# Filter spectra finished inside the convolution, and the gate work moved beside it, in a hybrid encoder layer

## The chip, the core and the metric

The kernel runs on one core of a Trainium2 chip. The metric is device microseconds of that core for one execution; of several executions the median is given. A profile is one further execution, recorded by the hardware profiler; its span runs from the first to the last instruction.

## The reference, cut to what matters

```python
u = rms_norm(h); P = u @ W_in                     # 2048 x 1024 rows; 10 blocks of 512 columns
# Hyena group, 512 channels: v, x1, x2 = conv3(P[:, :1536])
filt = sin_ffn(positions) @ w3 * exp(-t*|deltas|)  # order 2, two directions, length L = 2048
spec = rfft(concat(fwd, 0, flipped bwd))           # length 2L
for o, gate in enumerate((x1, x2)):
    z = gate * (irfft(rfft(z, 2L) * spec[:, o])[:L] + z * skip[o])
# mLSTM group, 4 heads x 128, both directions, from q, k, v, o and gates:
F = cumsum(log_f); m_t = running max; w = exp(...)   # the gates' scans
C = carry_decay * C + we * k v^T                     # states, chunk by chunk
h = (s @ v + inter * q @ C) / max(|den|, exp(-m_t))
# then group norms, output projection, cross-attention (256 memory rows), squared-ReLU MLP
```

## The kernel before, in words

**Numbers.** Most matrix products are done in three passes on split operands (a high and a low part, `wh`/`wl` and `xh`/`xl`, split at L366; the matmuls are L361 to L363, written mm<-xh,wh and so on in the profile). Products of the convolution and of the mLSTM are plain fp32 products, which the profile shows as two matmul records each.

**The convolution** runs as a two-stage transform of 4096 points: a product over 32 or 64 rows of time (`f1`), a store to DRAM that regroups the rows, and a product with one 128 x 128 matrix per pair of frequencies (`dm`). The way back is one product per frequency block (`em`), a store and load through DRAM, and a product with `e2`. Rows go through DRAM in `fs` (filters), `zs` (signal), `zg` (back) and `hd` (finished filter spectra).

**The stages**, in the order of the program (L1845):

1. `filters` (L231), woven with the sweeps over the first columns of W_in: per position pair and order, two products w3 (L177/L185), windows (DVE, POOL), the front (L294: two full 128 x 128 products, L297) and a store to `fs`; then 32 blocks (L323 to L346), each with two `dm` products (L344), copies and a store to `hd`.
2. `hyena` (L812), woven with the remaining sweeps and the `natural` projections: `load1` and `spectrum` (L896) of the signal; then per order 16 frequency steps, each with loads of signal rows and finished spectra (`load2`), copies that double the spectrum over both halves of the partitions (`double`, L862), two `dm` products (L926), the complex product (L928 and L929 on ACT, L930 and L932 on DVE, L931 on POOL) and, one product late, the way back (L892). Then the inverse in eight steps (`load3`, `e2`): for the first order in two column tiles beside each other (L177/L185), for the second as two full products (L949).
3. `mlstm` (L967) begins with the gates: one load of the gate columns (L991), transposes (L998), scans of seven doubling steps each (L1019/L1020), a loop of 62 dependent steps on single values (L1046/L1048), exponentials, and transposes back (L1038, L1052, L1073, L1074). It goes on with 15 backward states (`update`, L1093). Both are woven with `memproj`, the projections of the memory, which holds three of the `natural` blocks.
4. Sixteen chunks (L1162) woven with `memproj`'s end and with the attention; then the MLP.

**What sets the order.** A generator yields after each piece of work; `weave` (L1827) draws from two generators in turn by their yields and the two totals given to it. On top of that a scheduler places each instruction in the queue of its engine, so that the order on an engine differs from the order of the code. Each engine works through its queue in order. `beside` (L173) issues two products that use different parts of the array.

Of the kernel before, what the change touches and what calls it, by code (L numbers as in the profile page):

```python
# [18 lines left out]
L = 2048  # L19
# [8 lines left out]
def shape_constants():  # L28
# [15 lines left out]
    c_win = np.stack([win, winb], 0)  # L44
# [17 lines left out]
    f1h = np.zeros((2, 2, 32, 2, 64))  # L62
    e2h = np.zeros((2, 2, 2, 64, 128))
    for h in range(4):
        f1h[h // 2, h % 2, :, h % 2] = own
        e2h[0, h // 2, h % 2, :, 32 * h:32 * h + 32] = inv
        e2h[1, h // 2, h % 2, :, h::4] = inv
# [9 lines left out]
    for par in range(2):  # L77
# [12 lines left out]
    dm = dm.reshape(32, 128, 128)  # L90
# [7 lines left out]
        "c_f1": f1.transpose(1, 0, 2),  # L98
        "c_f1h": f1h.reshape(128, 128),
        "c_e2h": e2h.reshape(4, 128, 128).transpose(1, 0, 2),  # L100
# [34 lines left out]
class Prog:  # L135
# [37 lines left out]
    def beside(self, first, second):  # L173
        n = self.banks.index(first[0].tensor.name)
        n = self.banks.index(first[0].tensor.name)
        held = self.banks[max(0, n - 4):max(0, n - 2)] if first[0].tensor.name != second[0].tensor.name else []
        b = self.nc.tensor.matmul(*second, start=True, stop=True)  # L177
        for i in reversed(self.nc.cur_bb.bb.instructions[-4000:]):
            own = [x.bass_ap.tensor.name for x in i.ins if getattr(x, "bass_ap", None) is not None]
            for t in [t for t in held if t in own]:  # L180
                held.remove(t)
                self.tc.add_manual_dep(b.ins, i.name, mybir.DependencyInfo(
                    mybir.DependencyClass.Sync, mybir.DependencyReason.DATA), reason="beside")
        with self.tc.high_priority(2000):
            self.tc.keep_in_program_order(self.nc.tensor.matmul(*first, start=True, stop=True))  # L185
# [45 lines left out]
    def filters(self):  # L231
        nc, tc, a = self.nc, self.tc, self.a
        sd = [self.dram(f"fs{o}", (2, 128, 16, CH)) for o in range(2)]
        hd = self.dram("hd", (2, 32, 128, CH))
        sb, ta, tb = self.fsb, self.ta, self.tb
        if True:
# [4 lines left out]
            f1 = sb.tile([128, 2, 128], F32, name="f1")  # L241
            nc.scalar.dma_start(out=f1, in_=a["c_f1"])

            def sine(dst, src, b, fr, first=False):
# [11 lines left out]
                nc.scalar.activation(dst, u if len(dst.shape) == 2 else u.rearrange("p (q j) -> p q j", j=16), AF.Sin)  # L256

            hid = sb.tile([128, 16, 128], F32, name="hid")
            for c in range(4):
# [10 lines left out]
                sine(hid[:, :, 32 * c:32 * c + 32].rearrange("p j q -> p q j"), p2, 2, 3)  # L270
# [23 lines left out]
            def front(e, st, jj, o, js):  # L294
                for p in range(2):
                    pp = self.hy()
                    nc.tensor.matmul(pp, f1[:, p], e[p], start=True, stop=True)  # L297
                    nc.scalar.copy(st[p][:, jj], pp)
                    if jj == 1:
                        nc.sync.dma_start(out=sd[o][p, :, js], in_=st[p])  # L300

            nxt = windows(0)
            for j2 in range(8):
                js = slice(2 * j2, 2 * j2 + 2)
                yield 14
# [17 lines left out]
            def blocks(o, i):  # L323
                p, k = divmod(2 * i, 16)
                dm = sb.tile([128, 2, 128], F32, tag="dm", name="dm", bufs=3)
                d = nc.sync.dma_start(out=dm, in_=a["c_dm"][:, 2 * i:2 * i + 2])
                if o == 0 and i < 3:
                    tc.keep_in_program_order(d)
                t = ta()
                nc.sync.dma_start(out=t, in_=sd[o][p, 8 * k:8 * k + 16].rearrange("(k r) j c -> (r j) k c", k=2))  # L330
                return dm, t

            order = [(o, i) for o in range(2) for i in range(16)]
            q = [blocks(*order[0]), blocks(*order[1])]
            for n, (o, i) in enumerate(order):
                if True:
                    yield 3.4
                    dm, t = q.pop(0)
                    if n + 2 < 32:
                        q.append(blocks(*order[n + 2]))  # L340
                    hs = ta()
                    for m in range(2):
                        pp = self.hy()
                        nc.tensor.matmul(pp, dm[:, m], t[:, m], start=True, stop=True)  # L344
                        nc.scalar.copy(hs[:, m], pp)
                    nc.sync.dma_start(out=hd[o, 2 * i:2 * i + 2].rearrange("k l c -> l k c"), in_=hs)  # L346
# [59 lines left out]
    NAT_AT = (0, 2, 4)  # L406

    def inproj_open(self, es):
# [21 lines left out]
        for i in range(8):  # L430
            mem += ([nat[i // 2]] if i in self.NAT_AT else []) + first[i + 1:i + 2] + second[i:i + 1]
        items = tr[:4] * 2 + tr[4:] + [nat[c] for c in (3, 0, 1, 2)] + tr[4:] + [nat[3]] + mem
# [190 lines left out]
    def memproj(self):  # L623
# [45 lines left out]
        for i in range(8):  # L669
            if i in self.NAT_AT:  # L670
                yield from self.natural(0, (i // 2,))
# [140 lines left out]
    def hyena(self, es):  # L812
        nc, tc, a = self.nc, self.tc, self.a
        hy = self.dram("hy", (3, L, CH)).rearrange("s (n h j) c -> s h n j c", h=4, j=16)
        hq = self.dram("hy", (3, L, CH)).rearrange("s (q j) c -> s q j c", j=16)
        hd = self.dram("hd", (2, 32, 128, CH))
        yh = self.dram("yh", (L, CH)).rearrange("(q j) c -> q j c", j=16)
        sds = [self.dram(f"zs{o}", (32, 2, 4, 16, CH)) for o in range(2)]
        gds = [self.dram(f"zg{o}", (32, 2, 4, 16, CH)) for o in range(2)]

        def by_time(t, s, js):
            for h in range(4):
                nc.sync.dma_start(out=t[32 * h:32 * h + 32], in_=hy[s, h, :, js])

        def by_block(d, i):
            return d[2 * i:2 * i + 2].rearrange("k r h j c -> (r h j) k c")

        def by_pair(d, b, js):
            v = d.rearrange("k r h j c -> h (k r) j c")
            return [(slice(64 * g, 64 * g + 64), v[2 * b + g, :, js]) for g in range(2)]  # L830
# [9 lines left out]
        e2 = sb.tile([128, 4, 128], F32, name="e2")  # L840
        nc.sync.dma_start(out=f1, in_=a["c_f1h"])
        nc.sync.dma_start(out=e2, in_=a["c_e2h"])
        ghy = self.bcast(sb, a["hy_norm_g"], CH, "ghy")
        def load1(j2):
            z = ta()
            js = slice(2 * j2, 2 * j2 + 2)
            by_time(z, 0, js)
            return z

        def load2(o, i):  # L850
            dm = sb.tile([128, 2, 128], F32, tag="dm", name="dm", bufs=2)
            em = sb.tile([128, 2, 128], F32, tag="em", name="em", bufs=2)
            nc.sync.dma_start(out=dm, in_=a["c_dm"][:, 2 * i:2 * i + 2])
            nc.sync.dma_start(out=em, in_=a["c_em"][:, 2 * i:2 * i + 2])
            t, hr, hi = ta(), ta(), ta()
            nc.sync.dma_start(out=t, in_=by_block(sds[o], i))
            src = hd[o, 2 * i:2 * i + 2].rearrange("k (r l) c -> r l k c", r=2)
            nc.sync.dma_start(out=hr[0:64], in_=src[0])
            nc.sync.dma_start(out=hi[64:128], in_=src[1])
            return dm, em, t, hr, hi  # L860

        def double(i, hr, hi):  # L862
            nc.scalar.copy(hr[64:128], hr[0:64])
            if i == 0:
                nc.scalar.copy(hr[64:65, 0], hi[64:65, 0])
                nc.vector.memset(hi[64:65, 0], 0.0)
            nc.vector.tensor_copy(hi[0:64], hi[64:128])

        def load3(o, j2):
            js = slice(2 * j2, 2 * j2 + 2)  # L870
            r = [ta() for p in range(2)]
            for b in range(2):
                for own, d in by_pair(gds[o], b, js):
                    nc.sync.dma_start(out=r[b][own], in_=d)
            gate = ta()
            if o:
                nc.sync.dma_start(out=gate, in_=hq[2, :, js])
            else:
                by_time(gate, 1, js)
# [10 lines left out]
        def back(m, em, y, gs, dst):  # L890
# [3 lines left out]
            if m == 1:  # L894
                nc.scalar.dma_start(out=dst, in_=gs)

        def spectrum(o, j2, z):
            st = [ta() for p in range(2)]
            for jj in range(2):
                pp = [self.hy() for b in range(2)]  # L900
                self.beside(*((pp[b], f1[64 * b:64 * b + 64], z[64 * b:64 * b + 64, jj]) for b in range(2)))
                for b in range(2):
                    (nc.vector.tensor_copy if b else nc.scalar.copy)(st[b][:, jj], pp[b])
            for b in range(2):
                for own, d in by_pair(sds[o], b, slice(2 * j2, 2 * j2 + 2)):
                    (nc.sync if b else nc.scalar).dma_start(out=d, in_=st[b][own])

        q = [load1(0), load1(1)]
        for j2 in range(8):
            yield 3.5  # L910
# [3 lines left out]
        for o in range(2):  # L914
            gd = gds[o]
            nxt = load2(o, 0)
            for i in range(16):
                yield 3.5
                dm, em, t, hr, hi = nxt
                if i < 15:  # L920
                    nxt = load2(o, i + 1)
                gs = ta()
                double(i, hr, hi)
                for m in range(2):
# [8 lines left out]
                    late(lambda m=m, em=em, y=y, gs=gs, dst=by_block(gd, i): back(m, em, y, gs, dst))  # L933
            late(None)
            nxt = load3(o, 0)
            for j2 in range(8):
                yield 3.5 if o else 7.0
# [4 lines left out]
                for jj in range(2):  # L942
                    pp = self.hy()
                    if o == 0:
                        own = [slice(64 * b, 64 * b + 64) for b in range(2)]
                        self.beside(*((pp[own[b]], e2[:, b, own[b]], r[b][:, jj]) for b in range(2)))
                    else:
                        for p in range(2):
                            nc.tensor.matmul(pp, e2[:, 2 + p], r[p][:, jj], start=p == 0, stop=p == 1)  # L949
# [14 lines left out]
                nc.sync.dma_start(out=yh[:, js], in_=sq)  # L964
            late(None)

    def mlstm(self, es):  # L967
        nc, tc, a = self.nc, self.tc, self.a
# [949 lines left out]
```

## Time and profile before

| | |
|---|---|
| median of 3 runs | 3288.78 us (3285.28 to 3291.98) |
| profiled execution | 3292.63 us, span 3290.9 us, mean granted clock 0.975 |
| PE busy | 3097.7 us (94%), 15113 matmul records |
| DVE, ACT, POOL busy | 1971.7 us (60%), 1502.7 us (46%), 1242.2 us (38%) |
| DMA | 655.75 MB, mean 199 GB/s |

Matmuls are pipelined and their ends are modelled, so a busy PE is not PE at its peak. The stages lie in the span as follows: filters to 470 us, signal spectrum to 548, frequency steps and inverses to about 1108, gates, backward states and memory projections to 1346, and the rest (chunks, attention, MLP) to the end.

### The profile page before, as it was taken

The numbers are of one execution on the slowest core, as the hardware profiler recorded it, in microseconds if no ns is written. First come the engines' busy times: TensorE is split into PE (matmuls) and PEld (weight loads), VectorE is DVE, ScalarE is ACT, GpSimd is POOL, SyncE is SP. The second block draws the span as 40 slices with busy tenths as digits, with TensorE's granted clock in tenths as the row PEclk, the third lists the DMA queues.
The fourth block names the chain that finished last, engine by engine and source line by source line (L and its number), as shares of the span: only waits on it lengthen the run. The fifth ranks groups of instructions, "written<-read, shape, count | busy, mean of one in ns | idle before, by whom it ended". The sixth has DMA issues, their size and how long they took to land.

```text
span 3290.9 us, 45063 instructions
## 1 busy us (share of the span) xinstructions
PE 3097.7 (94%) x15113; PEld 2470.2 (75%) x15113; DVE 1971.7 (60%) x3316; ACT 1502.7 (46%) x2842; POOL 1242.2 (38%) x863
## 2 busy tenths in 40 slices
PE   7999999898999996799999998999999999999998
PEld 5656665674667885698988896888788887888876
DVE  7765224535556664676766556665755686565695
ACT  5533445643663343444444435545555543333335
POOL 0122000210222214534433106886756574434483
PEclk9999999999999997899999999999999999999999
DMA  5554998888787679758465526664644475444434
GB/s 188 187 201 148 313 307 257 261 240 249 215 246 231 200 250 309 210 164 262 140 223 196 195 78 225 207 219 160 218 156 157 157 234 166 132 140 140 130 96 163
DMA packets 473903, 655.75 MB, mean 199 GB/s; under 512 B 41278, under 2 KB 253374, under 8 KB 472648
## 3 DMA queue, kind: packets, MB, share of 16 engines
q1 hardware_dynamic: 437796, 594.30, 58.0%
q10 hardware_dynamic: 35876, 58.57, 5.2%
q8 instruction: 120, 1.97, 0.3%
q14 instruction: 111, 0.91, 0.1%
HBM read 437.73 MB, written 214.99 MB: 198 GB/s over the span
## 4 chain that ended last, share of the span: by engine, by line
PE 66%; DMA 14%; DVE 8%; issue 5%; ACT 3%; POOL 2%; SPq 1%; ACTq 0%; DVEq 0%; POOLq 0%
PE mm L361 14%; PE mm L363 13%; PE mm L362 13%; PE hy L363 5%; PE hy L361 5%; PE hy L362 5%; DVE wl L366 2%; PE hy L344 2%; DMA rw<-rows 2%; PE hy L297 2%; DMA wn<-in_w_in_dram 1%; DMA a<-zg 1%; DMA a<-hd 1%; PE hy L177 1%; PE hy L892 1%
## 5 line engine op out<-in xcount | busy, mean ns | idle before, releaser
L366 DVE TENSOR_TENSOR wl<-wn,wh 128x512 fp32r<-128x512 f32 (+1 forms) x364 | 285.9, 820 | 147.8 <-ACT wh L366 144.0
L1499 DVE TENSOR_TENSOR bl<-wr,bh 128x512 fp32r<-128x512 f32 x213 | 239.0, 1129 | 125.2 <-ACT bh L1498 125.1
L1498 ACT CAST ah<-w 128x512 fp32r<-128x512 f32 x284 | 176.5, 623 | 301.2 <-PE hy L362 153.4
L366 ACT CAST wh<-wn 128x512 fp32r<-128x512 f32 (+1 forms) x364 | 209.3, 619 | 211.6 <-DMA wn<-in_w_in_dram 57.9
L931 POOL TENSOR_TENSOR b<-b,a 128x512 f32<-128x512 f32 x64 | 88.6, 1384 | 574.4 <-ACT b L929 406.2
L361 PE MATMUL mm<-xh,wh 128*128 128x512 f32 x640 | 278.0, 436 | 12.3 <-ACT xh L366 5.5
L362 PE MATMUL mm<-xl,wh 128*128 128x512 f32 x640 | 270.2, 423 | 2.2 <-DVE xl L366 1.6
L363 PE MATMUL mm<-xh,wl 128*128 128x512 f32 x640 | 263.2, 411 | 0.0
L1499 DVE TENSOR_TENSOR al<-w,ah 128x512 fp32r<-128x512 f32 x236 | 226.0, 959 | 61.4 <-ACT ah L1498 61.1
L1498 ACT CAST bh<-wr 128x512 fp32r<-128x512 f32 x232 | 143.9, 622 | 231.9 <-PE mm L363 173.9
L363 PE MATMUL mm<-bh,al 128*128 128x512 f32 x576 | 225.4, 394 | 7.6 <-DVE al L1499 4.4
L361 PE MATMUL mm<-bh,ah 128*128 128x512 f32 x576 | 227.0, 394 | 0.9 <-DVE u L1624 0.8
L362 PE MATMUL mm<-bl,ah 128*128 128x512 f32 x576 | 226.1, 393 | 0.0
L361 PE MATMUL mm<-act,wh 128*128 128x512 f32 x512 | 200.4, 395 | 2.9 <-ACT wh L366 2.9
L362 PE MATMUL mm<-act,wh 128*128 128x512 f32 x512 | 200.8, 392 | 0.0
L363 PE MATMUL mm<-act,wl 128*128 128x512 f32 x512 | 199.6, 393 | 0.1
L1355 POOL TENSOR_TENSOR ssum<-ssum,sq 128x512 f32<-128x512 f32 x56 | 80.3, 1433 | 274.5 <-ACT sq L1354 274.5
L361 PEld LDWEIGHTS mm<-xh,wh 128*128 128x128 f32 x640 | 123.0, 192 | 71.8 <-issue 29.9
L361 PE MATMUL hy<-bh,ah 128*128 128x512 f32 x448 | 175.2, 391 | 0.0
L362 PE MATMUL hy<-bl,ah 128*128 128x512 f32 x448 | 174.6, 390 | 0.0
L363 PE MATMUL hy<-bh,al 128*128 128x512 f32 x448 | 174.4, 390 | 0.0
L362 PEld LDWEIGHTS mm<-xl,wh 128*128 128x128 f32 x640 | 122.7, 192 | 53.8 <-issue 26.2
(368 smaller groups left out, 8785.5 us busy)
## 6 DMA issues: line engine op xcount, KB each, us to landing
wr<-hc SPq DMA_DIRECT2D x224, 256.0 KB
w<-in_ff_w_dram SPq DMA_DIRECT2D x176, 256.0 KB
hc<-t SPq DMA_DIRECT2D x128, 256.0 KB
wn<-in_w_in_dram SPq DMA_DIRECT2D x100, 256.0 KB
hc<-q SPq DMA_DIRECT2D x96, 256.0 KB
fs<-a SPq DMA_DIRECT2D x32, 512.0 KB
a<-fs SPq DMA_DIRECT2D x32, 512.0 KB
hd<-a SPq DMA_DIRECT2D x32, 512.0 KB
```

The lines of the kernel that those rows point to most:

```text
L177: b = self.nc.tensor.matmul(*second, start=True, stop=True)
L297: nc.tensor.matmul(pp, f1[:, p], e[p], start=True, stop=True)
L344: nc.tensor.matmul(pp, dm[:, m], t[:, m], start=True, stop=True)
L361: mm(ps, lh, rh, start=start, stop=False)
L362: mm(ps, lh, rl, start=False, stop=False)
L363: mm(ps, ll, rh, start=False, stop=stop)
L366: both = (self.nc.scalar.copy(hi, src), self.nc.vector.tensor_tensor(lo, src, hi.bitcast(F32), ALU.subtract))
L892: nc.tensor.matmul(pg, em[:, m], y, start=True, stop=True)
L931: nc.gpsimd.tensor_tensor(xt, xt, hi[:, m], ALU.mult)
L1355: nc.gpsimd.tensor_tensor(ssum, ssum, sq, ALU.add)
L1498: self.nc.scalar.copy(hi, src)
L1499: eng.tensor_tensor(lo, src, hi.bitcast(F32), ALU.subtract)
```

## The change

1. The front of the filters becomes four 64 x 64 products (two halves of the contraction, two halves of the output, into two banks) instead of two full products; constants and the rows in DRAM are laid out for it. `beside` takes any number of products. Loads and stores by time become two DMAs instead of four, and stores and loads by pair one instead of two or more; the store of the way back becomes two.
2. The 32 blocks at the end of `filters` go, and `hd` and `double` with them. In `hyena`, `load_filter` loads `dm` and the rows of `fs` two steps ahead, and `response` makes the finished spectrum one step ahead, with two copies on ACT and two on DVE per product.
3. The inverse of the second order uses the two column tiles too.
4. The gates become a generator of their own in the weave with the convolution, between `natural(0, (3,))` and `sweep(range(4, 10), 0)`. Two `natural` blocks move from `memproj` into that weave. The totals and some yields of the weaves change.
5. `update`, the sum of the directions and the last scaling of a chunk become fused DVE operations on 128 x 129 or 128 x 128 pieces; the product `ve` of the backward states goes from DVE to POOL.

```diff
 def front(e, st, jj, o, js):
+    pp = [self.hy() for p in range(2)]
+    self.beside(*((pp[p][64 * (p ^ g):64 * (p ^ g) + 64], f1[64 * g:64 * g + 64, 64 * p:64 * p + 64],
+                   e[p][64 * g:64 * g + 64]) for p in range(2) for g in range(2)))
     for p in range(2):
-        nc.tensor.matmul(pp, f1[:, p], e[p], start=True, stop=True)
...
+        def response(i, dm, t):
+            hr, hi = ta(), ta()
+            for m in range(2):
+                pp = self.mm()
+                nc.tensor.matmul(pp, dm[:, m], t[:, m], start=True, stop=True)
+                nc.scalar.copy(hr[0:64, m], pp[0:64])
+                nc.scalar.copy(hr[64:128, m], pp[0:64])
+                nc.vector.tensor_copy(hi[64:128, m], pp[64:128])
+                nc.vector.tensor_copy(hi[0:64, m], pp[64:128])
...
-                            nc.tensor.matmul(pp, e2[:, 2 + p], r[p][:, jj], start=p == 0, stop=p == 1)
+                    self.beside(*((pp[own[g]], e2, r[g][:, jj]) for g in range(2)))
...
-                nc.gpsimd.tensor_tensor(new, old, bc(DC, r), ALU.mult)
-                    nc.vector.tensor_tensor(nv, nv, pc[:, 0:258], ALU.add)
+                    nc.vector.scalar_tensor_tensor(new[:, h], old[:, h], DC[:, r + h:r + h + 1],
+                                                   pc[:, 129 * i:129 * i + 129], ALU.mult, ALU.add)
...
-            weave(p.filters(), s, 230, 200)
+            weave(p.filters(), s, 80, 200)
...
-                            p.sweep(range(4, 10), 0, False), p.natural(0, (3,), p.prep_mem, 2)),
-                      227, 382)
+                            p.natural(0, (3,)), p.gates(), p.sweep(range(4, 10), 0, False),
+                            p.natural(0, (0, 1), p.prep_mem, 2)),
+                      271, 420)
...
-            for _ in take(n, 3):
-                pass
-            weave(n, take(m, 20), 138, 105)
+            weave(n, take(m, 20), 132, 95)
```

In the changed kernel's own lines the transposes of the gates are L965 (columns in), L1005 (ends of the scans), L1019 and L1040/L1041 (back); the three passes are L336 to L338, a pair of `beside` L175/L184, a state's product L1088, a chunk's L1136 to L1176.

On PE, at the gates of the kernel before, this is how the transposes of the loop's result (L1052) and of `G` (L1073) stand:

```order
L362 MATMUL mm_10166<-wl_9794,xh_83 128x256
L363 MATMUL mm_10166<-wh_9793,xl_84 128x256
L361 MATMUL mm_10166<-wh_9793,xh_83 128x256
L1052 MATMUL hy_9016<-ident_60,mm_8951 128x1
L1073 MATMUL hy_9037<-ident_60,G_8924 128x128
L1052 MATMUL hy_9016<-ident_60,mm_8951 128x1
```

On PE, the same place of the changed kernel (`arr` is the gate columns, `ends` the last values of both scans, `mm` the loop's result, `G`, `ed` and `we` what goes back; `e2` marks the first inverse):

```order
L338 MATMUL mm_6154<-wh_5487,xl_84 128x272
L965 MATMUL hy_6195<-ident_60,arr0_6191 128x128
L965 MATMUL hy_6201<-ident_60,arr1_6192 128x128
L1005 MATMUL hy_6257<-ident_60,ends_6251 1x128 x2
L1019 MATMUL hy_6326<-ident_60,mm_6261 128x1
L1040 MATMUL hy_6347<-ident_60,G_6234 128x128
L175 MATMUL hy_6372<-a_6031,e2_2697 64x512
L184 MATMUL hy_6372<-a_6030,e2_2697 64x512
L175 MATMUL hy_6376<-a_6031,e2_2697 64x512
L184 MATMUL hy_6376<-a_6030,e2_2697 64x512
L1019 MATMUL hy_6326<-ident_60,mm_6261 128x1
L1040 MATMUL hy_6347<-ident_60,ed_6342 128x128
```

All of the gates' transposes moved together: before, 345 rows of projections lie between the first and the last of them, now four rows of the inverse.

On DVE, two products of a frequency step of the kernel before:

```order
L930 TENSOR_TENSOR b_3675<-hy_3672,a_3584 128x512
L932 TENSOR_TENSOR b_3675<-b_3675,b_3674 128x512
L930 TENSOR_TENSOR b_3688<-hy_3685,a_3584 128x512
L867 COPY a_3665<-a_3665 64x1024
L932 TENSOR_TENSOR b_3688<-b_3688,b_3687 128x512
```

On DVE, two products of a frequency step of the changed kernel (L914 and L916 are the former L930 and L932):

```order
L914 TENSOR_TENSOR b_3503<-hy_3500,a_3384 128x512
L843 COPY a_3486<-mm_3487 64x512
L844 COPY a_3486<-mm_3487 64x512
L680 MEMSET P_3580 128x1
L916 TENSOR_TENSOR b_3503<-b_3503,b_3502 128x512
L843 COPY a_3486<-mm_3493 64x512
L844 COPY a_3486<-mm_3493 64x512
L914 TENSOR_TENSOR b_3517<-hy_3514,a_3384 128x512
L916 TENSOR_TENSOR b_3517<-b_3517,b_3516 128x512
```

The one copy of 64 x 1024 became four of 64 x 512, which stand between the two operations of the first product and ahead of the second.

On PE, a chunk of the kernel before (L1101 states, L1147 scores, L1185/L1187 the outputs):

```order
L1101 MATMUL hy_10706<-ve_10703,kn_10645 128x129 x2
L1101 MATMUL hy_10710<-ve_10703,kn_10645 128x129 x2
L1147 MATMUL hy_10742<-qn_10721,kk_t_10722 128x128 x4
L1185 MATMUL hy_10762<-va_10502,rw_10505 128x129
L1187 MATMUL hy_10762<-cf_10702,rw_10507 128x129
```

On PE, the same chunk of the changed kernel (`mm<-wl,kt` are passes of `memproj`):

```order
L1088 MATMUL hy_10749<-ve_10742,kn_10683 128x129 x2
L337 MATMUL mm_11117<-wl_11030,kt_10845 128x512
L338 MATMUL mm_11117<-wh_11029,kt_10845 128x512
L1136 MATMUL hy_10910<-qn_10761,kk_t_10762 128x128 x4
L1174 MATMUL hy_10930<-va_10668,rw_10671 128x129
L336 MATMUL mm_11127<-wh_11029,kt_10845 128x512
```

Passes of `memproj` now stand between a chunk's products, up to the fourth chunk.

More of the change, by code (lines that the diff above doesn't have):

```diff
@@ L171, in hy, with beside @@
         return t
[L173 to L177, printed above, removed]
+    def beside(self, *products):
+        names = [p[0].tensor.name for p in products]
+        n = min(self.banks.index(t) for t in names)
+        held = self.banks[max(0, n - 4):max(0, n - 2)] if len(set(names)) > 1 else []
+        b = self.nc.tensor.matmul(*products[-1], start=True, stop=True)
         for i in reversed(self.nc.cur_bb.bb.instructions[-4000:]):
@@ L184, in beside @@
         with self.tc.high_priority(2000):
-            self.tc.keep_in_program_order(self.nc.tensor.matmul(*first, start=True, stop=True))
+            for p in reversed(products[:-1]):
+                self.tc.keep_in_program_order(self.nc.tensor.matmul(*p, start=True, stop=True))
     def dram(self, name, shape):
@@ L322, in filters @@
             late(None)
[L323 to L346, printed above, removed]
         self.fes.close()
@@ L670, in memproj @@
             if i in self.NAT_AT:
[L671 removed]
+                yield from self.natural(0, (self.NAT_AT[i],))
             yield 11
@@ L846, in load1, with load_filter @@
             js = slice(2 * j2, 2 * j2 + 2)
-            by_time(z, 0, js)
-            return z
+            for g in range(2):
+                nc.sync.dma_start(out=z[own[g]], in_=hy[0, g, :, js])
+            return z
+        def load_filter(o, i):
+            dm = sb.tile([128, 2, 128], F32, tag="dm", name="dm", bufs=3)
+            nc.sync.dma_start(out=dm, in_=a["c_dm"][:, 2 * i:2 * i + 2])
+            p, k = divmod(2 * i, 16)
+            t = ta()
+            for g in range(2):
+                nc.sync.dma_start(out=t[own[g]], in_=of_block(fs[o][p, 64 * (p ^ g):64 * (p ^ g) + 64], k))
+            return dm, t
@@ L858, in load2 @@
[L858 to L867, printed above, removed]
+            t = ta()
+            for g in range(2):
+                nc.sync.dma_start(out=t[own[g]], in_=of_block(sds[o][g], 2 * i))
@@ new lines, in load2 @@
+            return em, t
+        def response(i, dm, t):
[7 more added lines that the diff above has]
+                nc.vector.tensor_copy(hi[0:64, m], pp[64:128])
+                if i == 0 and m == 0:
+                    nc.scalar.copy(hr[64:65, 0], pp[64:65])
+                    for r in range(2):
+                        nc.vector.memset(hi[64 * r:64 * r + 1, 0], 0.0)
+            return dm, hr, hi
@@ L894, in back @@
             if m == 1:
-                nc.scalar.dma_start(out=dst, in_=gs)
+                for g in range(2):
+                    nc.scalar.dma_start(out=of_block(dst[g], 2 * i), in_=gs[own[g]])
         def spectrum(o, j2, z):
```

201 lines of the change are left out of this document (97 added, 104 removed).

## The prediction

> **What bounds the kernel now.** I read the windows of the stages first (window, us, then busy time and count of PE, its weight loads, DVE, ACT and POOL, the granted clock, the DMA share and GB/s):
>
> ```profile
> 0.00:470.00 470.00, 435.54 (x1632) 283.70 (x1633) 256.21 (x454) 212.79 (x367) 56.94 (x38) 0.97 0.66 223
> 470.00:548.00 78.00, 72.96 (x298) 47.64 (x297) 31.27 (x46) 31.41 (x47) 0.00 (x0) 1.00 0.88 247
> 548.00:1108.00 560.00, 517.78 (x2533) 372.59 (x2532) 303.15 (x501) 278.44 (x454) 118.69 (x83) 0.97 0.83 243
> 1108.00:1346.00 238.00, 183.61 (x1262) 169.00 (x1260) 130.78 (x377) 93.98 (x230) 80.38 (x66) 0.89 0.79 246
> 1346.00:3291.00 1945.00, 1887.79 (x9392) 1597.23 (x9392) 1250.28 (x1940) 886.07 (x1747) 986.23 (x677) 0.99 0.55 173
> ```
>
> PE is busy for 92 to 97% of four windows; no other engine reaches two thirds, and DMA is short of full. So in these the work on PE sets the time, and a stage is forecast by adding up what PE issues. The fourth is different: 54 us without PE, a clock of 0.89, and DMA at 0.79. Two pieces of it, with the DMA of the whole stage:
>
> ```profile
> 1191.00:1283.00 92.00, 74.14 (x475) 66.52 (x474) 48.13 (x101) 30.90 (x65) 27.73 (x22) 0.87 0.98 304
> 1283.00:1346.00 63.00, 36.73 (x219) 33.25 (x217) 30.39 (x95) 22.90 (x94) 43.99 (x35) 0.78 0.82 259
> DMA packets 55264, 58.64 MB, mean 246 GB/s; under 512 B 5640, under 2 KB 38664, under 8 KB 55244
> ```
>
> At 304 GB/s DMA is full (0.98). In the second piece PE is idle for 26 of 63 us: the first chunks stand alone there.
>
> The prices on PE are distances between starts, not durations, as matmuls overlap. A split pass of 512 columns, one of 256 columns, and a pair of column tiles:
>
> ```profile
> 198.61 0.39 PE L363 MATMUL mm<-xh,wl 128*128 128x512 f32 x1
> 198.84 0.39 PE L361 MATMUL mm<-xh,wh 128*128 128x512 f32 x1
> ...
> 711.01 0.28 PE L362 MATMUL mm<-wl,xh 128*128 128x256 f32 x1
> 711.13 0.28 PE L363 MATMUL mm<-wh,xl 128*128 128x256 f32 x1
> 711.34 0.64 PE L177 MATMUL hy<-a,e 128*64 128x512 f32 x1
> 711.34 0.64 PE L185 MATMUL hy<-a,e 128*64 128x512 f32 x1
> 711.82 0.59 PE L177 MATMUL hy<-a,e 128*64 128x512 f32 x1
> ```
>
> That is 0.23, 0.12, and 0.43 to 0.48 for two records that start together. A full fp32 product, from the chain that ended last (start, us) and the groups of the first window:
>
> ```profile
> 358.26 1.72 PE hy L344 x4
> ...
> L297 PE MATMUL hy<-b,f 128*128 128x512 f32 x128 | 65.5, 624 | 0.0
> L344 PE MATMUL hy<-a,dm 128*128 128x512 f32 x128 | 62.2, 592 | 0.0
> ```
>
> 1.72 us for four records is 0.43 each, 0.86 a product; fronts and blocks have 128 records each.
>
> **The change part by part.** I counted the rows of PE in the order of both programs between the same marks (last filter, last signal product, last inverse, first free chunk) and priced them so.
>
> *Filters, 470 us.* The blocks go from here: 128 x 0.43 = -55. They are not saved: the same 64 products come back as `response`, +55 in the frequency steps. The fronts: 64 products become 64 x 2 quadrant products in groups of four. Two quadrants of one row tile each are the row tiles that already run at once:
>
> ```profile
> 200.75 0.69 PE L177 MATMUL hy<-fw,hid 64*128 64x512 f32 x1
> 200.75 0.69 PE L185 MATMUL hy<-fw,hid 64*128 64x512 f32 x1
> ```
>
> Row tiles start together here into two banks, and column tiles above into one. If four quadrants start together, two full products (1.72) become 0.86: 32 x -0.86 = -27.5; if only two do, 0. I take -27.5, as both halves of the condition show in rows. [...] Sweep passes move on to later stages (141 of them, six steps, at 0.23: -32.3), with 3.4 of transposes. 470 - 55 - 27.5 - 32.3 - 3.4 = 352.
>
> *Signal spectrum, 78 us.* Another 146 sweep passes leave (-33.3). By PE alone 46 would be left; but 12 of the pairs now stand in one run with little beside them, and this stage moves 19 MB at 247 GB/s before, some 16 after, which is 55 us at the rates of 247 to 304 above. I take 55 (48 to 66).
>
> *Frequency steps and inverses, 560 us.* Sweeps and projections moved in, +82.3 (32.3 + 33.3 from above, the rest two `natural` blocks); responses +55; the second inverse in column tiles, 32 x 0.86 to 16 x 0.86, -13.8; transposes +3.4. Sum 687. DMA, at 0.83 here, brings about the same rows (`fs` in place of `hd`) over a longer time, so that waits for it should not grow.
>
> To this comes what the order shows at the gates. They are now all but in one piece on PE, and their DVE rows stand in one piece too. PE works in order, so it waits through the chain from the load to the last transpose, with two inverse pairs (1.7 us) as its only work. The rows, first the load, the scans (L1019/L1020), the loop (L1046/L1048) and the last copy:
>
> ```profile
> 1136.12 0.38 SPq L991 DMA_DIRECT2D gts<-gt  x1
> ...
> 1140.54 0.50 DVE L996 COPY arr<-gts 128x64 f32<-128x64 f32 x4 [3.09 <-DMA gts<-gt]
> ...
> 1145.77 0.29 DVE L1026 TENSOR_TENSOR rw<-rw,ab 128x128 f32<-128x128 f32 x1 [3.18 <-ACT ab L1006]
> ...
> 1146.36 0.28 DVE L1019 TENSOR_TENSOR pad<-pad 64x128 f32<-64x128 f32 x1
> 1146.67 0.29 DVE L1020 TENSOR_TENSOR pad<-pad 64x128 f32<-64x128 f32 x1
> ...
> 1184.28 0.22 DVE L1048 TENSOR_TENSOR mm<-mm,er 1x4 f32<-1x4 f32 x2
> 1184.46 0.23 DVE L1046 TENSOR_TENSOR mm<-mm,er 1x4 f32<-1x4 f32 x2
> ...
> 1190.56 0.69 DVE L1075 COPY cols<-hy 128x512 f32<-128x512 f32 x1 [4.53 <-PE hy L1074]
> ```
>
> Load to data 4.4, and the store that it waits for up to as much again; data to the logarithm's end 5.5 (1140.5 to 1146.0); two scans of 14 steps at 0.31 with their copies, 10.2; the loop, 62 steps at 0.09 (two in 0.18), 5.6; the tail at most 6.5 (1184.7, where the loop ends, to 1191.2, with other work in it), taken at half, 3.3. With 1 for small copies that is 30 to 34, less 1.7, plus 2 for the clock: after a wait matmuls come at half speed, as at the load of `zg`:
>
> ```profile
> 1014.64 3.78 PE L949 MATMUL hy<-a,e 128*128 128x512 f32 x4 [2.76 <-DMA a<-zg]
> ...
> 1018.67 0.43 PE L363 MATMUL mm<-wh,xl 128*128 128x272 f32 x1
> 1018.89 0.43 PE L361 MATMUL mm<-wh,xh 128*128 128x272 f32 x1
> ...
> 1020.73 0.29 PE L362 MATMUL mm<-wl,xh 128*128 128x272 f32 x1
> 1020.86 0.29 PE L363 MATMUL mm<-wh,xl 128*128 128x272 f32 x1
> ```
>
> (0.22 between starts, then 0.13.) [...] I take +34. Before, the same chain stood among projections and cost PE little.
>
> The frequency step on the other engines (busy, mean ns of one):
>
> ```profile
> L903 DVE COPY a<-hy 128x512 f32<-128x512 f32 x16 | 11.0, 687 | 5.2 <-PE hy L185 5.2
> L867 DVE COPY a<-a 64x1024 f32<-64x1024 f32 x32 | 22.1, 690 | 58.0 <-DMA a<-hd 50.0 <-DMA em<-in_c_em_dram 3.6 <-DMA kn<-st 2.8
> ...
> L928 ACT ACTIVATE b<-hy 64x512 f32<-64x512 f32 x64 | 38.2, 596 | 8.2 <-PE hy L926 3.6 <-ACT a L893 1.9 <-DVE b L930 0.6
> L929 ACT COPY b<-hy 64x512 f32<-64x512 f32 x64 | 37.1, 579 | 0.7
> L931 POOL TENSOR_TENSOR b<-b,a 128x512 f32<-128x512 f32 x64 | 88.6, 1384 | 574.4 <-ACT b L929 406.2 <-DVE a L867 135.3 <-DVE wl L366 11.1
> L932 DVE TENSOR_TENSOR b<-b 128x512 f32<-128x512 f32 x64 | 45.2, 707 | 25.5 <-POOL b L931 25.3
> ...
> L892 PE MATMUL hy<-b,em 128*128 128x512 f32 x128 | 67.5, 609 | 12.3 <-DVE b L932 9.5 <-issue 1.7 <-ACT st L802 1.0
> ```
>
> A step gains four copies of 512 columns on DVE (4 x 0.69) and loses one (0.69), +2.1 x 32 = 66 on DVE; ACT gains four at 0.58 and loses one of 64 x 1024. DVE has 257 us free in this window, so this costs nothing as long as the way back (L892) finds its `y`. The chain behind a frequency product is 0.60 + 0.58 + 1.38 + 0.71 = 3.3, with four copies in front of it 6.1; the passes that cover it, some 24 x 0.23 and two products of 0.86, last 7.2. It holds on the mean, and I take +4 for places where it does not. 687 + 34 + 4 = 725.
>
> *Gates, backward states and memory, 238 us.* Its PE work goes from 169.5 by my count to 152, as two projections leave. Its gates are gone from it, chunks 0 to 3 have passes between them, and and a state's work on DVE and POOL is fused. What binds then is the loads: 58.6 MB less the two projections' share, about 53 MB, at 304 GB/s 174 us, and 11 for a start without full queues: 185 (170 by no lean start; 205 if a third of the old idle time stays).
>
> *The rest, 1945 us.* PE fills 97%; a chunk's DVE work is fused, POOL's falls, and neither is waited for by much: -2.
>
> **Sum.** 352 + 55 + 725 + 185 + 1943 = 3260, against 3290.9: -31. The profiled execution took 1.7 more than its span, and the median was 3.9 below that execution: 3260 + 1.7 - 3.9 = 3258. A measurement of this kernel can tell about 0.2% (6.6 us) from no change.
>
> **The rivals.**
>
> *Row tiles take turns at a bank.* Then the fronts cost what they did: +27.5, 3286, no change. [...] 0.15.
>
> *Slower: the frequency step's chain is longer than its cover.* The place is L892's successor and the two DVE operations with copies in between. At 6.1 against 7.2 there is 1.1 us to spare; if ACT's four copies and two evacuations stand ahead of the two operations too (2 x 0.58 more), the chain passes its cover, and 64 products waiting 1.2 each cost 77: 3335. It decides from a chain of 7.2 us on. For it: L892 waited 9.5 us for L932 already, with fewer copies. Against: responses are a step ahead. 0.14.
>
> *The gates' wait is not lost.* While PE waits, DMA brings the weights and rows that the next steps would wait for, and the sweeps that follow have no waits of their own (before, PE was without work for 42 us of that window): -25, 3233. Against it, prefetching is limited by buffers. 0.13.
>
> *The convolution's waits halve.* With more sweep work beside the steps and four loads made into two, half of these 42 us goes, and the fourth stage comes to 170: -40 with some of the spectrum's, 3218. 0.15.
>
> That leaves 0.43 for the forecast. That the change does not do what it says is part of the forecast already: the gates are in the same weave as the convolution, but not beside it on PE.
>
> **How the numbers follow.** The forecast's own bounds are -7 and +11 (spectrum), -15 and +20 (fourth stage), -8 and +4 (gates), together about 3235 to 3283. Reaching to the third and fourth rival and above the first gives 3205 to 3305; the slower rival is left out. Faster by over 0.2%: all but the top of the forecast, both faster rivals and a third of the first, 0.40 + 0.28 + 0.05 = 0.73. Slower: its rival and bits of the first and the forecast, 0.16. No change, 0.11.
>
> **What would show it.** Four records of the front that start together (two by two: first rival). PE idle for 30 to 36 us between the last `natural(0, (3,))` pass and the first inverse, with L1005 waiting for DVE. Waits of L871 (the former L892) for L916 below 15 us in all; above 60, the slower rival. The stage from the last inverse to chunk 5 at 170 to 205 us with a clock above 0.93. PE-bound filters of 352 us. The forecast is wrong if PE keeps full through the gates, or if the spectrum's run of pairs waits longer than 15 us.

## The result and the profile after

The changed kernel takes 3261.32 us (median of 4, 3256.08 to 3272.3) against 3288.79; the ratio is 0.9919, 95% interval 0.9900 to 0.9939. The forecast was 3258. The profiled execution took 3256.08 us, span 3254.4, with a clock of 0.975 as before.

The windows of the same five stages in the changed kernel (columns as before), and the piece of the third that holds the gates:

```profile
0.00:355.00 355.00, 325.37 (x1460) 207.61 (x1460) 241.63 (x441) 161.48 (x284) 58.08 (x38) 0.99 0.55 180
355.00:418.40 63.40, 52.04 (x207) 31.38 (x204) 24.40 (x38) 22.06 (x37) 0.00 (x0) 0.92 0.94 305
418.40:1105.00 686.60, 630.83 (x3079) 454.63 (x3078) 404.55 (x750) 347.44 (x591) 118.69 (x83) 0.96 0.70 202
1105.00:1313.00 208.00, 164.34 (x1106) 152.13 (x1105) 112.12 (x292) 83.53 (x222) 67.33 (x56) 0.87 0.90 280
1313.00:3254.40 1941.40, 1884.03 (x9399) 1594.71 (x9397) 1246.02 (x2018) 884.57 (x1737) 938.25 (x641) 0.99 0.55 174
...
741.00:780.00 39.00, 7.30 (x25) 2.64 (x23) 22.87 (x121) 8.52 (x15) 0.00 (x0) 0.60 0.23 61
```

| stage | before | forecast | after |
|---|---|---|---|
| filters | 470 | 352 | 355 |
| signal spectrum | 78 | 55 | 63.4 |
| frequency steps, inverses (and now gates) | 560 | 725 | 686.6 |
| states, memory (before, gates too) | 238 | 185 | 208 |
| rest | 1945 | 1943 | 1941.4 |
| span | 3290.9 | 3260 | 3254.4 |

The sum came out; three of its terms did not. The frequency steps are 38 us shorter than forecast, the stage behind them 23 longer and the spectrum 8. For 39 us at the gates PE works 7, as the order had shown, and DMA moves 61 GB/s (share 0.23). PE's own waits in the third stage (line, releaser: us in all, times, longest):

```profile
PE hy L1005 <- DVE ends L1001: 14.3, 2, 9.7
PE hy L965 <- DVE arr L963: 8.6, 1, 8.6
PE mm L840 <- DMA a<-fs: 7.2, 1, 7.2
PE hy L1019 <- DVE mm L1015: 6.1, 1, 6.1
PE mm L336 <- ACT st L199: 4.1, 1, 4.1
PE hy L871 <- DVE b L916: 2.2, 1, 2.2
...
PE hy L1040 <- ACT ed L1036: 2.0, 1, 2.0
```

The rows of the gates (L965, L1005, L1019, L1040) add up to 31.0, and the way back (L871, formerly L892) waits 2.2 for its operand where it waited 9.5. What the slower rival needs is not there. The bytes fell neither in the spectrum's stage (first line; 19.30 MB before) nor, by more than 0.45 MB, in the fourth:

```profile
DMA packets 9628, 19.33 MB, mean 305 GB/s; under 512 B 1073, under 2 KB 4940, under 8 KB 9623
...
DMA packets 51516, 58.19 MB, mean 280 GB/s; under 512 B 3539, under 2 KB 33952, under 8 KB 51497
```

### The profile page after: what moved, and what is told of

The parts are those of the page before. It is cut to its first block, busy times and chain, and to the rows that moved or that the text cites. A ratio compares the mean times of both kernels' runs of the same rounds, so it can differ in the third digit from the quotient of the medians.

```text
span 3254.4 us, 45314 instructions
## 1 busy us (share of the span) xinstructions
PE 3056.6 (94%) x15241; PEld 2440.5 (75%) x15241; DVE 2028.7 (62%) x3535; ACT 1499.1 (46%) x2870; POOL 1182.3 (36%) x818
## 4 chain that ended last, share of the span: by engine, by line
PE 73%; DMA 10%; DVE 8%; issue 5%; ACT 2%; POOL 1%; SPq 1%; ACTq 0%; DVEq 0%; POOLq 0%
PE mm L338 16%; PE mm L336 16%; PE mm L337 16%; PE hy L338 5%; PE hy L337 5%; PE hy L336 5%; PE hy L175 3%; PE hy L871 1%; PE mm L840 1%; PE hy L910 1%; DVE bl L1491 1%; DMA xt<-in_x_t_dram 1%; DVE wl L341 1%; DMA va<-vd 1%; PE hy L1174 1%
## 5 line engine op out<-in xcount | busy, mean ns | idle before, releaser
L341 DVE TENSOR_TENSOR wl<-wn,wh 128x512 fp32r<-128x512 f32 (+1 forms) x364 | 272.9, 785 | 110.5 <-ACT wh L341 107.9
L336 PE MATMUL mm<-xh,wh 128*128 128x512 f32 x640 | 276.9, 434 | 3.0 <-ACT xh L496 3.0
L337 PE MATMUL mm<-xl,wh 128*128 128x512 f32 x640 | 256.4, 401 | 1.3 <-DVE xl L341 1.3
L338 PE MATMUL mm<-xh,wl 128*128 128x512 f32 x640 | 256.2, 401 | 0.0
L338 PE MATMUL mm<-bh,al 128*128 128x512 f32 x576 | 224.3, 392 | 7.8 <-DVE al L1491 5.2
L336 PE MATMUL mm<-bh,ah 128*128 128x512 f32 x576 | 225.7, 392 | 1.0 <-DVE u L1616 0.9
L336 PE MATMUL mm<-act,wh 128*128 128x512 f32 x512 | 200.4, 395 | 4.4 <-ACT wh L341 4.4
L338 PE MATMUL mm<-act,wl 128*128 128x512 f32 x512 | 200.2, 394 | 2.0 <-DVE wl L341 2.0
L336 PE MATMUL hy<-bh,ah 128*128 128x512 f32 x448 | 175.2, 391 | 0.0
L338 PE MATMUL hy<-bh,al 128*128 128x512 f32 x448 | 174.4, 390 | 0.0
L336 PEld LDWEIGHTS mm<-xh,wh 128*128 128x128 f32 x640 | 121.5, 190 | 63.3 <-issue 33.4
L319 POOL TENSOR_TENSOR b<-b 128x512 f32<-128x512 f32 x32 | 57.4, 1793 | 292.8 <-DVE b L314 133.2
```

The costliest lines, as they stand in the source:

```text
L319: nc.gpsimd.tensor_tensor(e[1], f, b, ALU.subtract)
L336: mm(ps, lh, rh, start=start, stop=False)
L337: mm(ps, lh, rl, start=False, stop=False)
L338: mm(ps, ll, rh, start=False, stop=stop)
L341: both = (self.nc.scalar.copy(hi, src), self.nc.vector.tensor_tensor(lo, src, hi.bitcast(F32), ALU.subtract))
```

## The experiments

All are edits of the changed kernel. Medians, with the ratio to the kernel before (the changed kernel: 3261.3, 0.9919). The kernel before stood at 3292.5 beside the first four runs of the table and at 3288.0 beside the others, so the ratios compare them better than the medians. Each interval is some 6 us either way; by that, an estimate, two runs are clearly apart from about 9 us (0.003) on.

| run | us | ratio, 95% interval |
|---|---|---|
| full front | 3271.4 | 0.9944 (0.9927 to 0.9961) |
| full inverse | 3259.2 | 0.9909 (0.9889 to 0.9928) |
| gates back | 3257.2 | 0.9894 (0.9874 to 0.9914) |
| gates in pieces | 3237.7 | 0.9836 (0.9816 to 0.9856) |
| copies twice | 3277.9 | 0.9971 (0.9958 to 0.9984) |
| more loads | 3272.7 | 0.9954 (0.9939 to 0.9970) |
| traffic back | 3257.3 | 0.9912 (0.9883 to 0.9940) |
| pieces and a projection | 3222.5 | 0.9809 (0.9785 to 0.9832) |

**The front as full products.**

```diff
-                self.beside(*((pp[p][64 * (p ^ g):64 * (p ^ g) + 64], ...) for p in range(2) for g in range(2)))
+                for p in range(2):
+                    nc.tensor.matmul(pp[p], full[:, p], e[p], start=True, stop=True)
```

> The changed kernel with the front of the filters as two full products with zeros in the other quadrants, as before, in place of four quadrants that start together. Theory of the prediction: the filters are bound by PE, and 64 full products cost 55 us where the quadrants cost 27.5, so the filters take 382 us instead of 355 and the kernel 27 more, about 3288. Rival: the fronts hide beside the windows of DVE and POOL, and the time stays within 5 us of 3261.

The last product of the front starts at 368.8 us instead of 354.6: 14 us. (In the eight kernels whose filters are those of the change it starts between 353.9 and 357.2.) The median rises by 10, by the ratios 8. Neither theory's number: the quadrants do save time, but half of what was forecast. That four of them start together, two row tiles in each of two banks, stands in the timeline of PE in the changed kernel:

```profile
209.49 0.40 PE L337 MATMUL mm<-xl,wh 128*128 128x512 f32 x1
209.82 0.64 PE L175 MATMUL hy<-b,f 64*64 64x512 f32 x1
209.82 0.65 PE L184 MATMUL hy<-b,f 64*64 64x512 f32 x3
210.30 0.59 PE L175 MATMUL hy<-b,f 64*64 64x512 f32 x1
210.31 0.60 PE L184 MATMUL hy<-b,f 64*64 64x512 f32 x3
210.84 0.50 PE L338 MATMUL mm<-xh,wl 128*128 128x512 f32 x1
211.17 0.40 PE L336 MATMUL mm<-xh,wh 128*128 128x512 f32 x1
```

A group (two such sets, as an fp32 product is two records) takes 1.02 us to the next pass; that pass takes 0.33 to its successor, and the pass ahead of the group 0.33, where passes among themselves take 0.23. So a group alone between passes costs 1.02 + 0.10 + 0.10 = 1.22 us. The two full products that it replaces stand like this in the kernel with the full front:

```profile
324.12 0.39 PE L344 MATMUL mm<-xh,wl 128*128 128x512 f32 x1
324.35 1.88 PE L301 MATMUL hy<-b,full 128*128 128x512 f32 x4
325.66 0.79 PE L342 MATMUL mm<-xh,wh 128*128 128x512 f32 x1
326.29 0.40 PE L343 MATMUL mm<-xl,wh 128*128 128x512 f32 x1
```

From 324.35 to 326.29 are 1.94 us; less one pass (0.23) that is 1.71 for two products, 0.86 each, as forecast. The difference of 0.49 a group makes 15.7 us for 32, where 14 were measured. Two more kernels, one profiled execution each (3284.9 and 3307.9 us), issue both forms twice.

```diff
+                for r in range(2):
-                self.beside(*(...))
+                    self.beside(*(...))
```

> The changed kernel with each group of four quadrants in the front issued twice into the same banks, 32 groups more. The last quadrant of the filters starts at 354.6 us without them. Theory that four quadrants cost what two records of a full product cost (0.86 a group): it starts at 382. Theory from undoing the quadrants, which brought 14 us where 27.5 were forecast, that a group costs about 1.3 instead: at 396.

The last quadrant starts at 373.5, 18.9 later; in the order of PE 29 passes fewer (0.23 each) stand ahead of it, so 32 groups cost about 25.5, 0.80 each. That is rough, as PE's waits in the filters changed by 3 us too. Where two groups follow each other, their timeline reads:

```profile
223.44 0.64 PE L175 MATMUL hy<-b,f 64*64 64x512 f32 x1
223.44 0.65 PE L184 MATMUL hy<-b,f 64*64 64x512 f32 x3
...
224.34 0.59 PE L175 MATMUL hy<-b,f 64*64 64x512 f32 x1
224.35 0.60 PE L184 MATMUL hy<-b,f 64*64 64x512 f32 x3
...
224.77 0.59 PE L175 MATMUL hy<-b,f 64*64 64x512 f32 x1
```

0.42 to 0.43 from one set of four records to the next, 0.86 a group, as forecast: the theory of 1.3 a group falls for a group inside a run. A group alone between passes pays some 0.36 more (1.22 less 0.86), for entering and leaving.

```diff
                 for p in range(2):
-                    nc.tensor.matmul(pp[p], full[:, p], e[p], start=True, stop=True)
+                    for r in range(2):
+                        nc.tensor.matmul(pp[p], full[:, p], e[p], start=True, stop=True)
```

> The kernel with full products in the front, each of them issued twice into the same bank, 64 full products more. The last one starts at 368.8 us without them. Theory that a full product costs 0.86 where it stands: at 424. Theory that full products cost less here than their distance in the chain, about 0.65, and the quadrants what was forecast: at 410.

The last one starts at 408.1, 39.3 later, with 36 passes fewer ahead of it (8.2): 47.5 for 64 products. Three other things changed: eight transposes fewer (0.9) stand ahead, the first front starts 1.1 us earlier, and from the first w3 product on PE has no idle time where it had 4.0. With these it is 53.5, 0.84 each, which agrees with the 0.86 of the rows above; that the last start lies near the second theory's 410 comes from the work that moved. So one size was off: a full product costs 0.86 as forecast, a group of quadrants 0.86 only inside a run and 1.22 alone.

**The second inverse as full products.**

```diff
-                    self.beside(*((pp[own[g]], e2, r[g][:, jj]) for g in range(2)))
+                    if o == 0:
+                        self.beside(*((pp[own[g]], e2, r[g][:, jj]) for g in range(2)))
+                    else:
+                        for g in range(2):
+                            nc.tensor.matmul(pp, ef[:, g], r[g][:, jj], start=g == 0, stop=g == 1)
```

> The changed kernel with the inverse of the second order as two full products (a column tile filled up with zeros) that add into one bank. Theory of the prediction: 32 products of 0.86 us in place of 16 pairs of 0.86, +13.8 us, about 3275. Rival: this inverse waits for its rows or for the norm behind it, so that PE has room, and the time changes by under 4 us.

The total changes by 2 us, so the rival's number holds, but not its reason. Windows of this kernel, third and fourth stage:

```profile
422.00:1119.00 697.00, 644.45 (x3084) 464.55 (x3082) 406.29 (x750) 347.50 (x591) 116.29 (x83) 0.96 0.69 200
1119.00:1319.00 200.00, 154.46 (x1102) 141.53 (x1101) 107.67 (x291) 83.77 (x222) 68.06 (x56) 0.93 0.92 287
```

The third stage grows by 10 and PE's busy time by 14, as the theory says; the fourth shrinks by 8, to 200, where the runs that leave that stage alone have 205 to 210. So in this run what the column tiles gain at the end of the convolution is given back behind it. That loads ran ahead during the longer inverse is the likely reason, not tried.

**The gates back at the start of the mLSTM.**

```diff
-                            p.natural(0, (3,)), p.gates(), p.sweep(range(4, 10), 0, False),
+                            p.natural(0, (3,)), p.sweep(range(4, 10), 0, False),
...
-            m = p.mlstm(ms)
+            m = chain(p.gates(), p.mlstm(ms))
...
+            for _ in take(n, 3):
+                pass
```

> The changed kernel with the gates back at the start of the mLSTM, beside the memory projections. Theory that PE's wait at the gates is lost time: the 31 us of idle PE in the convolution go, the stage behind, which is bound by its loads, hides most of the chain again: about -25, 3236. Rival, that the wait is made up elsewhere (loads that run ahead, sweeps later): within 7 us of 3261, or slower by up to 15 as the states then wait for the gates.

```profile
421.00:1072.00 651.00, 625.24 (x3066) 450.73 (x3064) 383.72 (x633) 341.20 (x582) 118.99 (x83) 0.98 0.73 212
1072.00:1310.00 238.00, 169.22 (x1123) 153.21 (x1122) 124.86 (x413) 86.91 (x219) 62.69 (x54) 0.86 0.80 250
...
1094.00:1155.00 61.00, 54.26 (x396) 50.65 (x395) 42.72 (x156) 34.93 (x62) 0.95 (x4) 0.97 0.69 213
1160.00:1240.00 80.00, 45.85 (x268) 36.72 (x267) 31.93 (x93) 23.11 (x47) 21.99 (x19) 0.86 1.04 332
```

The third stage loses 36 us, the fourth gains 30 and stands at 238, where the kernel before had it. The total moves by 4 us (8 by the ratios), which is not clear of noise. Each place pays about 30 us for the same chain. The rival's number held, but the wait was not made up: it was paid elsewhere. In the fourth stage PE waits for none of the gates' transposes. But DMA is short of full (0.69) while the chain runs, from 1094 to 1155 us, and full behind it (1.04): the first load of a state is issued at 1155.4, right behind the stores of the gates' results, and PE then waits 18.7 us for one load of keys and 10.9 for others. The forecast for the theory (-25) missed, as the fourth stage did not hide the chain.

**The gates in nine pieces.**

```diff
-                            p.natural(0, (3,)), p.gates(), p.sweep(range(4, 10), 0, False),
+                            p.natural(0, (3,)), among(p.sweep(range(4, 10), 0, False), p.gates()),
...
+def among(a, g):
+    for v in a:
+        yield v
+        next(g, None)
...
+            yield 1
             G = sg.tile([128, 128], F32, name="G")
```

> The changed kernel with the gates cut into nine pieces, one ahead of each unit of 24 passes of the sweep that follows them, so that PE has 5.5 us of passes between its gate transposes. Theory that PE's wait is lost time: 31 us of idle PE at the gates fall to under 5, with the clock's restart, so about -28, 3233. Rival, that the wait is made up elsewhere: within 7 us of 3261.

```profile
420.00:1089.00 669.00, 633.35 (x3077) 455.40 (x3075) 407.49 (x747) 347.41 (x591) 119.76 (x83) 0.97 0.71 207
1089.00:1297.00 208.00, 165.57 (x1109) 153.01 (x1109) 109.58 (x294) 84.07 (x222) 69.11 (x56) 0.87 0.90 281
```

PE waits for none of the gates' transposes any more. The third stage loses 18, with 36 us without PE instead of 56: 31 us of waits went and 11 of others came. The fourth keeps its 208, and the median falls by 24 (27 by the ratios, 18 between the profiled executions). The wait was lost time; the third rival falls.

**Response copies on DVE twice.**

```diff
+                for r in range(2):
-                nc.vector.tensor_copy(hi[64:128, m], pp[64:128])
-                nc.vector.tensor_copy(hi[0:64, m], pp[64:128])
+                    nc.vector.tensor_copy(hi[64:128, m], pp[64:128])
+                    nc.vector.tensor_copy(hi[0:64, m], pp[64:128])
```

> The changed kernel with the four DVE copies of a filter response made twice: 128 more copies of 0.69 us, 88 us of DVE work in the frequency steps. Theory that DVE has room there and the way back finds its operand: at most 8 us more, under 3269. Rival, that the chain of a step stands at its cover and the copies in front of it count: 2.8 us on 32 steps, up to 88, with half of that 3305.

```profile
422.00:1129.00 707.00, 637.48 (x3080) 454.89 (x3079) 500.07 (x869) 347.15 (x593) 120.22 (x83) 0.96 0.67 196
```

Between the two: 88 us of copies cost 17 (third stage 707 instead of 686.6). The chain has room, but copies beyond those of the change show through in a fifth of their time. What the change's own 66 us of copies cost can't be read from this; at the same fifth it would be 13.

**More loads in the states** (`more` loads 256 KB of kn into a tile of its own).

```diff
+            more(n)
             yield 3
```

> The changed kernel with one load more of 256 KB, which nobody reads, in each of the 15 backward states: 3.9 MB more in the stage behind the convolution. Theory that this stage is bound by its transfers (280 GB/s, share 0.90): 3.9 MB at 280 GB/s, +14 us, about 3275. Rival, that it is bound by chains of work and PE's waits there only look like loads: within 4 us of 3261.

```profile
423.00:1111.00 688.00, 631.75 (x3080) 455.22 (x3079) 404.17 (x740) 347.37 (x591) 118.25 (x83) 0.96 0.70 201
1111.00:1326.00 215.00, 166.90 (x1103) 153.92 (x1101) 110.89 (x299) 81.45 (x212) 67.32 (x54) 0.88 0.90 281
...
DMA packets 52898, 60.45 MB, mean 281 GB/s; under 512 B 3727, under 2 KB 34325, under 8 KB 52879
```

+11 in the median (of 14), 7 of it in this stage: 215, where the runs that leave it alone have 205 to 210. Of the 3.9 MB only 2.3 moved inside the stage, at the same rate of 281 GB/s, which is 8 us. The stage is bound by its transfers, though PE is idle for 48 us in it (44 in the changed kernel).

**The traffic of the finished spectra back.**

```diff
+                for r, h in enumerate((hr, hi)):
+                    nc.sync.dma_start(out=hd[o, i, r], in_=h)
```

> The changed kernel with stores to DRAM of each finished response, one step after it was made, 33.5 MB in the frequency steps, as many bytes as the store and the load of the finished spectra that the change took out (nobody reads them). Theory that PE binds these steps: DMA's share there rises from 0.70 to 0.85 and the time by under 6 us. Rival, that the lower traffic is what cut PE's idle time outside the gates from 42 to 24 us: +15 to +25, about 3281.

```profile
423.00:1111.00 688.00, 630.80 (x3078) 454.03 (x3077) 405.98 (x748) 346.53 (x591) 118.67 (x83) 0.96 0.82 250
```

DMA's share is back at 0.82 and nothing is slower, so the lower share isn't what cut PE's idle time. Nor had the change saved bytes in this stage: 136.0 MB moved there before and 138.7 after, and the share fell because the stage is longer. What the fourth rival rested on, more sweep work beside the steps and fewer, larger loads, is not tried by this run.

**Pieces, and a projection back beside the states.**

```diff
-    NAT_AT = {0: 2}
+    NAT_AT = {0: 1, 2: 2}
...
-                            p.natural(0, (0, 1), p.prep_mem, 2)),
+                            p.natural(0, (0,), p.prep_mem, 2)),
...
```

> The kernel with the gates in nine pieces, and with one of the two projections that the change moved into the convolution back beside the states, where PE is idle for 40 us. Theory that the stage behind the convolution is bound by its loads: 8 us of PE work leave the convolution, and 1 MB of weights and 0.5 MB of stores come to that stage (5 us): -3 to -8 against the kernel with pieces, about 3232. Rival, that PE's work counts there too: no change, 3238.

```profile
420.00:1071.00 651.00, 616.10 (x2937) 437.44 (x2936) 406.71 (x745) 341.71 (x581) 119.53 (x83) 0.98 0.73 211
1071.00:1284.50 213.50, 178.08 (x1284) 167.94 (x1283) 116.07 (x299) 89.78 (x235) 67.67 (x56) 0.92 0.91 281
```

The median is 15 us under the kernel with pieces, by the ratios 9, with intervals that overlap, and the profiled span 13. The direction is the theory's, and the gain at or a little above the top of its -3 to -8. Against the kernel before it is about 65. 140 matmuls left the third stage, 17 us of PE's busy time, twice what was expected of them; the fourth stage takes them up for 5.5. It has the lowest median of all.

## Why the prediction was right, point by point

- **PE binds the filters.** Right: 355 for 352, PE busy for 235 of 239 us from the first w3 product on. The term of the fronts was mis-sized: -14 in place of -27.5, because a group of quadrants alone between passes costs 1.22 and not 0.86. That the total still fits is luck: the rest of the stage shrank by some 10 more than its terms. Half of that is idle time of PE (34.5 us before, 29.6 after); for the other half no reason was found.
- **Row tiles take turns at a bank.** Fell: the trace shows four quadrants, two row tiles in each bank, starting within 0.02 us (209.82 us in the changed kernel, and 223.44 where groups are issued twice). The 0.15 for this rival was the author's estimate: no row of the kernel before has two row tiles in one bank.
- **Signal spectrum**, 63 for 55: the step that failed is the number of bytes. 16 MB were forecast and 19.3 moved, as many as before, at 305 GB/s and a share of 0.94; PE waits 5.1 us for `hy` and 5.6 for `fs`. (The wait of 7.2 for `fs` in the list above is a later one, at the start of the second order.)
- **The gates**, +34: measured 31, at the place and by the engine that the order had shown. The clock fell with it: 0.60 over those 39 us, and 0.50 from 750 to 770. Behind the waits, pairs started 0.85 to 1.01 us apart from 772.50 to 782.67 us, and 0.43 apart at 783.26.
- **The inverse**, -13.8: right on PE (14 us of busy time, 10 of the stage), worth nothing clear of noise in the total.
- **Frequency steps**, 686.6 for 725: the main step that failed is that the stage keeps its old idle time. Outside the gates PE is idle for 25 us where it was 42; the way back's waits fell from 9.5 to 2.2. That is 17 of the 38. Another 14 are work: PE's busy time grew by 113 and not by 127, among others because 122 passes came out of the spectrum's stage and not 146. The last 7 are the gates (31 for 34) and the +4 for late copies, which did not show. A lower share of DMA is not the reason of the idle time. That no copy in the steps waits for a load of finished spectra any more is the likely one, argued only.
- **States and memory**, 208 for 185: the step that failed is the number of bytes. 58.2 MB moved where 53 were forecast, which at 304 GB/s is 17 of the 23 us; the rest is the rate, 280 and not 304 GB/s over the whole stage, for which 11 us were allowed and 16 were needed. The clock there is 0.87 and not above 0.93. Two projections left, but weights of the memory projections that used to be loaded ahead are now loaded in this stage (13 loads of `xa_wq_t` and 8 of `xa_wk`, before 8 and 4).
- **The slower rival** fell, with room of about four fifths of 88 us. **The third** fell with the pieces. **The fourth** was half right: the convolution's other waits did fall, 42 to 25 us, whether for its reasons is open, and the fourth stage did not follow.

The forecast of the time was 3 us off because -38 in one stage met +23 and +8 in two others. That closeness is luck. What held is that PE sets the time of the filters and that the gates' chain is lost time on PE; the two stages bound by transfers were forecast with too few bytes. Where the gain of 27 us comes from is located only in part: undoing the quadrants takes 10 of it back, undoing the new inverse or the gates' place nothing clear of noise; the move of the filter spectra and the fused operations were not undone.

## What to carry to other kernels

A stage with idle PE need not have room (here 44 us idle at a DMA share of 0.90, and 3.9 MB more cost 11 us): look at its transfers before work or waits are moved into it, and count with the loads that will move up into the place of those that leave (58.2 MB moved where 53 were forecast). Time gained just ahead of such a stage can be given back there, as in the one run on the second inverse (10 us there, 8 behind it); the 18 us gained earlier in the convolution were kept. The gates' chain of small operations cost PE 31.0 us of waits where its matmuls stood together in PE's queue, and the fourth stage 30 us where the next loads stood behind it; cut into pieces between independent matmuls, 18 to 24 of its 31 us came back. Price small products by where they stand: entering and leaving a group (0.36 us) took two fifths of the gain forecast for the quadrants (0.86 a group).

## What the runs showed of the hardware

Two row tiles wrote two halves of one PSUM bank at once: four quadrants started within 0.02 us, and where two groups follow each other the sets came 0.42 to 0.43 us apart, as pairs of row tiles into two banks do in a run of pairs (0.43, changed kernel, 783.26 to 783.69 us). Four 64 x 64 quadrants of an fp32 product cost 0.86 us inside a run of their kind and 1.22 alone between passes, while a full product cost 0.86 between passes and, by the 53.5 us for 64 of them, 0.84 issued twice. 33.5 MB more in 688 us, at a share of 0.82, cost nothing that could be measured, while 3.9 MB more at a share of 0.90 cost 11 us.
